# The gates' low one-hot tiles of the first token half, made by ScalarE instead of VectorE

## The chip, the cores and the metric

The kernel is one launch on one core of a Trainium2 chip. The metric is the device time of that launch in microseconds (us). The profile shows the engines by short names: PE (TensorE, matrix products), PEld (its weight loads), DVE (VectorE), ACT (ScalarE), POOL (GpSimd) and SP (the queue that issues most transfers).

## What is computed

One layer of a transformer on 1024 tokens of width 1024: attention in windows, a short convolution, gated merging, and then a layer of 16384 experts ("PEER"). For the change only the last part matters, cut to this:

```python
s = einsum('thpd,hpnd->thpn', qh, sub_keys)            # 8 heads, 2 key halves, 128 keys
s_top, i_top = top_k(s, 16)
cand = s_top[:, :, 0, :, None] + s_top[:, :, 1, None, :]
best, pos = top_k(cand, 16)                            # 8 x 16 = 128 experts for each token
idx = i1 * 128 + i2
g = softmax(best)
act = gelu(ue . t)                                     # rows of u_tab picked by idx
out = sum_k (g * act)_k * ve_k                         # rows of v_tab picked by idx
```

For most tokens the kernel runs every expert densely, and so it needs the gates as a dense table: for each token a 128 by 128 matrix G with G[i2, i1] equal to the sum of g over the token's 128 picks (i1, i2). One token's G is a product of two one-hot matrices: E2 (pick by i2) transposed, times E1 (pick by i1) scaled by the gate g of the pick.

## The kernel before

The 1024 tokens are two halves of 512, called half 0 and half 1 (`hf`). Half 0 is the first half. The stage that matters is woven from two streams by `run_side`: the main stream `stage2(1)` (gates, merging, mixing, normalization, queries and scores of half 1, most of it matrix products of 512 columns into PSUM banks) and the side stream `gates(0)`, which makes the gate tables of half 0. A scheduler then sets the order of instructions on each engine by readiness and its own costs, so a changed instruction moves others. Each engine runs its own list strictly in order.

`gates(0)` runs four times (one for each 128 tokens) a selection and a build. `select` works almost only on VectorE: the 16 best of the candidates by maximum, index and replace instructions, then four rounds of a comparison tile `eq`, whose second factor `fe` ScalarE widens. `slots` turns the three results (i1, i2, gate) on TensorE, so that picks lie on partitions and tokens on the free axis, and ScalarE copies them out as `ii` and `g16`.

`build_g` takes 8 tokens at a time (a round, 16 rounds in a build). For each round VectorE makes four float16 tiles of 128 by 1024: `e1` and `e2` (comparison of a ramp with i1 and i2, both named `e` in the rows), `ah` (e1 times the high part of the gate) and `al` (e1 times the low part; the gate is kept as two float16 numbers). `expand` then multiplies: for each token two products of 128 columns (e2 by ah, e2 by al), four tokens to a PSUM bank `fbank` of which there are two, and ScalarE evicts each bank into `ge`, 512 columns at a time. Every 16 tokens `ge` goes to memory by a transfer that GpSimd issues. The tiles e1, e2, ah and al have two buffers each.

In the main stream the names are: `sa` and `sgv` (ScalarE evicts sigmoids, VectorE multiplies them, GpSimd adds `sa`), `mh` and `ml` (halves of the merged result: ScalarE, GpSimd), `x` (residual), `sq` (squares: ScalarE, added up by GpSimd), `rstd` (reciprocal root), `h2h` and `h2l` (the normalized activations), `qqh`/`qql` (queries), `sl` (scores), `sv`/`si` (their 16 best). The tail of the stage is the maximum and index work of `scores` on VectorE; the dense expert loop begins with the product `ups` when the last `sl` has been evicted.

Of the kernel before, what the change touches and what calls it, by code (L numbers as in the profile page):

```python
# [8 lines left out]
F32 = mybir.dt.float32  # L9
F16 = mybir.dt.float16  # L10
# [3 lines left out]
AF = mybir.ActivationFunctionType  # L14
ALU = mybir.AluOpType
# [12 lines left out]
TB = 8  # L28
REP = 4
# [80 lines left out]
class K:  # L110
# [828 lines left out]
    def slots(self, t, hf):  # L939

        nc, p = self.nc, self.pg
        fig = self.sel[hf, t][1]
        pt = self.fbank()
        for i in range(3):
            nc.tensor.transpose(pt[:, i * 128:(i + 1) * 128], fig[:, i, :], self.id32)
        ii = p.tile([128, 256, REP], F16, name="ii", tag="ii", bufs=1)
        nc.scalar.activation(ii, pt[:, 0:256].unsqueeze(2).to_broadcast([128, 256, REP]), AF.Copy)
        g16 = p.tile([128, 2, 128, REP], F16, name="g16", tag="g16", bufs=1)
        self.split(pt[:, 256:384].unsqueeze(2).to_broadcast([128, 128, REP]), 4096.0, g16[:, 0], g16[:, 1])
        return ii.rearrange("p (a b) r -> p a b r", a=2), g16  # L950

    def build_g(self, t, hf):

        nc, p = self.nc, self.pg
        yield
        yield
        ii, g16 = self.slots(t, hf)
        yield
        late = []
        for q in range(128 // 16):  # L960
            ge = p.tile([128, 128, 16], F32, name="ge", tag="ge", bufs=self.ge_bufs)
            for sub in range(16 // TB):
                t0 = q * 16 + sub * TB
                ts = slice(t0, t0 + TB)

                def onehot(name, src, idx, op):
                    x = p.tile([128, TB, 128 // REP, REP], F16, name=name, tag=name, bufs=2)
                    nc.vector.tensor_tensor(x, src, idx[:, ts].unsqueeze(2).to_broadcast([128, TB, 128 // REP, REP]),
                                            op=op)
                    return x  # L970

                e1 = onehot("e1", self.iota, ii[:, 0], ALU.is_equal)
                ah = onehot("ah", e1, g16[:, 0], ALU.mult)
                al = onehot("al", e1, g16[:, 1], ALU.mult)
                e2 = onehot("e2", self.iota, ii[:, 1], ALU.is_equal)
                late.append((t, hf, q, sub, ge, ah, al, e2))
                if len(late) > 1:
                    self.expand(*late.pop(0))
                yield
        for x in late:  # L980
            self.expand(*x)
            yield
# [465 lines left out]
```

## Time and profile before

| | |
|---|---|
| median of 3 runs | 3120.34 us (3112.7 to 3122.46) |
| the profiled execution | 3120.57 us, span 3118.8 us |
| PE busy | 2913.7 us, 93% of the span |
| DVE busy | 2631.9 us, 84% |
| ACT busy | 1180.7 us, 38% |
| POOL busy | 1067.5 us, 34% |
| the changed stage (first `ii` to the first `ups`) | 740 to 1111 us |

The table shows averages over stages that differ. What the changed stage waits for has to be read in that stage; its length adds to the rest, since the dense loop behind it starts when it is over.

### The profile page before, as it was taken

What the parts mean: (1) busy time and instruction counts of PE and PEld (TensorE: products, weight loads), DVE (VectorE), ACT (ScalarE), POOL (GpSimd) and SP (SyncE); (2) the same over time, 40 slices, a digit from 0 to 9 for tenths busy, and PEclk for the clock granted to TensorE, in tenths of its full rate; (3) what the DMA queues carried; (4) which work ended last, traced back from release to release, by engine and by line L of the source; (5) the groups of instructions that cost most, each with busy time, mean ns of one, the idle gap of its engine ahead of it and who ended that gap; (6) DMA issues with size and microseconds to landing.
All of it is one profiled execution on the core that took longest, in us unless ns stands there. A gap on an engine that the chain in (4) does not pass through costs nothing. (4 is left out here: it accounts for less than half of the span.)

```text
span 3118.8 us, 49200 instructions
## 1 busy us (share of the span) xinstructions
PE 2913.7 (93%) x18685; PEld 1534.6 (49%) x18685; DVE 2631.9 (84%) x5438; ACT 1180.7 (38%) x1878; POOL 1067.5 (34%) x812
## 2 busy tenths in 40 slices
PE   6899999998899989999999999999999999999998
PEld 2455555444454444443444444344444456666665
DVE  7788666698899999899799988889988988777687
ACT  4744566333444332322333332333332333433332
POOL 2100011202231004444444544444444443444453
PEclk9999999999999999999999999999999999999999
DMA  6333334653445628898899998889898989999996
GB/s 218 95 110 111 112 116 152 234 183 136 174 191 196 234 87 307 280 317 303 303 316 335 345 325 297 295 318 342 315 335 304 336 287 341 328 323 326 333 321 225
DMA packets 327198, 795.75 MB, mean 255 GB/s; under 512 B 22961, under 2 KB 147249, under 8 KB 319793
## 3 DMA queue, kind: packets, MB, share of 16 engines
q1 hardware_dynamic: 222992, 397.25, 38.1%
q0 software_dynamic: 103968, 395.36, 34.8%
q8 instruction: 146, 2.39, 0.3%
q14 instruction: 92, 0.75, 0.1%
HBM read 696.31 MB, written 96.21 MB: 254 GB/s over the span
## 5 line engine op out<-in xcount | busy, mean ns | idle before, releaser
L904 POOL DMA_INDIRECT row<-u,ci x512 | 680.5, 1329 | 920.9 <-DVE row L67 685.0
L67 DVE SCALAR_TENSOR_TENSOR row<-row,hn 128x1024 f32<-128x1024 f32 x512 | 620.6, 1226 | 80.9 <-DMA row<-u,ci 75.0
L67 PE MATMUL res<-wdl,vh 128*128 128x128 f16 (+2 forms) x2176 | 629.3, 306 | 28.1 <-DVE wdl L67 28.0
L67 PEld LDWEIGHTS <-vh 128*128 128x128 f16 x5120 | 469.2, 98 | 340.0 <-issue 11.3
L67 PE MATMUL res<-wdh,vh 128*128 128x128 f16 (+2 forms) x2176 | 625.1, 306 | 3.3 <-ACT vh L1109 1.7
L67 PE MATMUL res<-wdh,vl 128*128 128x128 f16 (+2 forms) x2176 | 625.7, 306 | 0.8 <-DVE vl L67 0.8
L67 PE MATMUL ups<-h,uh 128*128 128x512 f16 x1952 | 589.8, 384 | 21.9 <-DVE acc L67 12.8
L67 PEld LDWEIGHTS <-whl 128*128 128x128 f16 x3288 | 315.1, 99 | 367.9 <-issue 41.9
L1109 ACT ACTIVATE vh<-v 128x1024 f16<-128x1024 f32 x248 | 258.4, 1052 | 484.9 <-DMA v<-v 433.6
L67 PE MATMUL ups<-h,ul 128*128 128x512 f16 x976 | 374.9, 384 | 21.1 <-DVE ul L67 21.1
L67 PE MATMUL bank<-hT,whl 128*128 128x512 f16 x1584 | 375.5, 386 | 15.7 <-ACT hT L331 5.7
L67 PEld LDWEIGHTS <-vl 128*128 128x128 f16 x2560 | 251.5, 98 | 205.0 <-issue 37.2
L67 DVE SCALAR_TENSOR_TENSOR vl<-v,vh 128x1024 f16<-128x1024 f32 x248 | 300.1, 1222 | 55.6 <-ACT vh L1109 53.1
L67 PEld LDWEIGHTS <-uh 128*128 128x128 f16 x1952 | 192.8, 99 | 258.0 <-issue 36.6
L904 POOL DMA_INDIRECT row<-v,ci x128 | 200.5, 1566 | 220.8 <-DVE racc L67 197.7
L140 ACT ACTIVATE uh<-u 128x1024 f16<-128x1024 f32 x122 | 128.4, 1052 | 311.1 <-PE ups L67 255.3
L1128 ACT ACTIVATE wdh<-gel 128x512 f16<-128x512 f32 x128 | 80.3, 629 | 371.4 <-DVE gel L67 353.3
L67 DVE SCALAR_TENSOR_TENSOR racc<-row,fig,racc 128x1024 f32<-128x1024 f32 x127 | 163.0, 1283 | 10.7 <-DMA row<-v,ci 9.7
L67 PEld LDWEIGHTS <-ul 128*128 128x128 f16 x976 | 96.6, 99 | 141.6 <-DVE ul L67 23.5
L67 DVE SCALAR_TENSOR_TENSOR ul<-u,uh 128x1024 f16<-128x1024 f32 x122 | 148.6, 1221 | 15.2 <-ACT uh L140 15.1
L67 PEld LDWEIGHTS <-e 128*128 128x128 f16 x1792 | 114.4, 99 | 94.4 <-issue 37.5
L67 DVE TENSOR_TENSOR e<-iotas,ii 128x1024 f16<-128x1024 f16 x224 | 145.4, 691 | 18.2 <-PE fbank L67 13.1
(230 smaller groups left out, 4192.6 us busy)
## 6 DMA issues: line engine op xcount, KB each, us to landing
v<-v SPq DMA_DIRECT2D x248, 512.0 KB, 6.5
u<-u_t SPq DMA_DIRECT2D x122, 512.0 KB, 6.7
gd<-ge POOLq DMA_DIRECT2D x32, 1024.0 KB, 4.4
gt<-gd SPq DMA_DIRECT2D x32, 1024.0 KB, 13.6
wm<-w_mod SPq DMA_DIRECT2D x48, 512.0 KB, 4.3
gd<-ge SPq DMA_DIRECT2D x24, 1024.0 KB, 8.6
gt<-gd SPq DMA_DIRECT2D x32, 768.0 KB, 11.0
w<-w_in SPq DMA_DIRECT2D x34, 512.0 KB, 4.2
```

Of the source, the lines that this page charges most:

```text
L67: r = f(*args, **kw)
L140: nc.scalar.activation(h, src, AF.Copy, scale=float(scale))
L904: self.nc.gpsimd.indirect_dma_start(out=r, out_offset=None, in_=tab, in_offset=bass.IndirectOffsetOnAxis(ap=ci[:, s:s + 1], axis=0))
L1109: nc.scalar.activation(vh, v32, AF.Copy, scale=16.0)
L1128: nc.scalar.activation(wh, ge, AF.Copy, scale=256.0)
```

## The change

For half 0 alone the low tile `al` is no longer one VectorE instruction for 8 tokens but eight ScalarE instructions, one for each token: a copy of 128 columns of e1, with the token's low part (`glo`, float32, one number for each partition) as the scale. `glo` is computed once for each build from 128 columns, where `g16`'s low half took 512. Half 1, built later beside the dense loop, is as before.

```diff
         g16 = p.tile([128, 2, 128, REP], F16, name="g16", tag="g16", bufs=1)
-        self.split(pt[:, 256:384].unsqueeze(2).to_broadcast([128, 128, REP]), 4096.0, g16[:, 0], g16[:, 1])
+        wide = pt[:, 256:384].unsqueeze(2).to_broadcast([128, 128, REP])
+        if hf:
+            self.split(wide, 4096.0, g16[:, 0], g16[:, 1])
+        else:
+            self.glo = p.tile([128, 128], F32, name="glo", tag="glo", bufs=2)
+            nc.scalar.activation(g16[:, 0], wide, AF.Copy, scale=4096.0)
+            self.lo(self.glo, pt[:, 256:384], 4096.0, g16[:, 0, :, 0])
...
                 e1 = onehot("e1", self.iota, ii[:, 0], ALU.is_equal)
                 ah = onehot("ah", e1, g16[:, 0], ALU.mult)
-                al = onehot("al", e1, g16[:, 1], ALU.mult)
+                if hf:
+                    al = onehot("al", e1, g16[:, 1], ALU.mult)
+                else:
+                    al = p.tile([128, TB, 128 // REP, REP], F16, name="al", tag="al", bufs=2)
+                    for u in range(TB):
+                        nc.scalar.activation(al[:, u], e1[:, u], AF.Copy, scale=self.glo[:, t0 + u:t0 + u + 1])
                 e2 = onehot("e2", self.iota, ii[:, 1], ALU.is_equal)
```

The scheduler's order moves with it. In the first build ScalarE (names: `g` is g16, `ii` the turned indices) had, before:

```order
L947 ACTIVATE ii<-fbank 128x1024
L140 ACTIVATE g_7630<-fbank 128x512
L715 ACT_TABLE_LOAD
L715 ACTIVATE sa<-bank 128x512
L994 ACTIVATE ge<-fbank 128x128x4 x6
L720 ACTIVATE sgv<-bank 128x512
L994 ACTIVATE ge<-fbank 128x128x4 x14
```

and has now:

```order
L947 ACTIVATE ii<-fbank 128x1024
L954 ACTIVATE g_7630<-fbank 128x512
L985 ACTIVATE al<-e_7668,glo 128x128 x8
L985 ACTIVATE al<-e_7683,glo 128x128 x8
L1005 ACTIVATE ge<-fbank 128x128x4 x2
L985 ACTIVATE al<-e_7719,glo 128x128 x8
L1005 ACTIVATE ge<-fbank 128x128x4 x2
L715 ACT_TABLE_LOAD
L715 ACTIVATE sa<-bank 128x512
L985 ACTIVATE al<-e_7784,glo 128x128 x8
L1005 ACTIVATE ge<-fbank 128x128x4 x2
```

Eight `al` stand ahead of every pair of `ge`, and the `al` of a round stand ahead of the `ge` of the round before it; the table load and `sa` come after two rounds.

On VectorE the fourth selection stood behind the third build (`fi` and `cand` begin a selection, `x` is the residual):

```order
L67 TENSOR_TENSOR ah<-e_9879,g_9332 128x1024
L67 TENSOR_TENSOR al<-e_9879,g_9332 128x1024
L67 TENSOR_TENSOR e_9908<-iotas,ii 128x1024
L67 TENSOR_TENSOR e_9914<-iotas,ii 128x1024
L67 TENSOR_TENSOR ah<-e_9908,g_9332 128x1024
L67 TENSOR_TENSOR al<-e_9908,g_9332 128x1024
L67 SCALAR_TENSOR_TENSOR x_9435<-bank,g1s,x_9435 128x512
L67 CAST fi<-si_3544 128x256
L67 TENSOR_TENSOR cand<-sv_3543 128x8x16
```

Now it stands inside the build, from its fifth round on:

```order
L67 TENSOR_TENSOR e_9750<-iotas,ii 128x1024
L67 CAST fi<-si_3544 128x256
L67 TENSOR_TENSOR cand<-sv_3543 128x8x16
L67 TENSOR_TENSOR cand<-sv_3543 128x8x8
L67 TENSOR_TENSOR cand<-sv_3543 128x8x5
L67 TENSOR_TENSOR cand<-sv_3543 128x8x4
L67 TENSOR_TENSOR cand<-sv_3543 128x8x3
L67 TENSOR_TENSOR ah<-e_9750,g_9558 128x1024
L67 TENSOR_TENSOR e_9763<-iotas,ii 128x1024
L67 TENSOR_TENSOR cand<-sv_3543 128x8x2 x3
L67 TENSOR_TENSOR cand<-sv_3543 128x8x8
L67 MAX best<-cand 128x8
```

All of the maximum and index work of the fourth selection, to the first `eq`, now lies between tiles of the third build; the second and the third selection still stand behind the build before them.

In the fourth build ScalarE had, in the middle of the build before:

```order
L994 ACTIVATE ge<-fbank 128x128x4 x2
L799 ACTIVATE hn<-bank 128x512
L994 ACTIVATE ge<-fbank 128x128x4 x8
L799 ACTIVATE hn<-bank 128x512
L994 ACTIVATE ge<-fbank 128x128x4 x6
L140 ACTIVATE qqh<-bank 128x512
L810 ACTIVATE sl<-bank 128x512
L994 ACTIVATE ge<-fbank 128x128x4 x4
L799 ACTIVATE hn<-bank 128x512
L994 ACTIVATE ge<-fbank 128x128x4 x4
L140 ACTIVATE qqh<-bank 128x512
```

and now, for about the same rounds:

```order
L1005 ACTIVATE ge<-fbank 128x128x4 x2
L331 ACTIVATE h2h_10541<-x_9683,b2s 128x512 x3
L799 ACTIVATE hn<-bank 128x512
L1005 ACTIVATE ge<-fbank 128x128x4 x2
L140 ACTIVATE qqh<-bank 128x512 x2
L985 ACTIVATE al<-e_11057,glo 128x128 x8
L985 ACTIVATE al<-e_11093,glo 128x128 x8
L1005 ACTIVATE ge<-fbank 128x128x4 x2
L985 ACTIVATE al<-e_11129,glo 128x128 x8
L1005 ACTIVATE ge<-fbank 128x128x4 x2
L985 ACTIVATE al<-e_11165,glo 128x128 x8
L1005 ACTIVATE ge<-fbank 128x128x4 x2
```

All eight `h2h` stood ahead of this build; now four are inside it, three of them here, and the evictions of the main stream (`hn`, `qqh`, `sl`) stand between groups of `al`.

On TensorE the products of 512 and 128 columns of the main stream between the first and the last one-hot product are, build by build, 95, 95, 102 and 149 before and 169, 141, 90 and 180 now. In the first build and most of the second ten of them stand between the sixteen one-hot products of one round and those of the next (six before). The third build has none in its last seven rounds and the fourth none in six rounds in its middle. Between the sums of the squares and the last turn (`slots`) ahead of the fourth build stand 34 products of 512 columns now.

## Rows read from the trace of the kernel before

**Rows 1.** Windows: from:to, length, busy PE PEld DVE ACT POOL, granted clock, DMA share, GB/s.

```profile
740.00:787.00 47.00, 39.97 (x346) 23.69 (x345) 40.32 (x67) 20.63 (x37) 13.78 (x9) 0.93 0.47 180
787.00:815.00 28.00, 25.08 (x132) 11.79 (x130) 26.05 (x113) 10.58 (x15) 5.28 (x5) 1.00 0.47 170
815.00:862.00 47.00, 40.45 (x347) 23.96 (x346) 40.73 (x69) 20.08 (x36) 13.98 (x10) 0.93 0.48 181
862.00:888.00 26.00, 23.98 (x123) 11.12 (x121) 24.95 (x112) 9.65 (x14) 3.12 (x4) 1.00 0.46 168
888.00:936.00 48.00, 43.27 (x361) 25.58 (x362) 44.83 (x70) 21.49 (x38) 20.74 (x11) 0.96 0.53 204
936.00:982.00 46.00, 40.73 (x191) 18.68 (x190) 42.15 (x132) 20.52 (x29) 8.54 (x6) 0.93 0.49 166
982.00:1028.00 46.00, 43.68 (x412) 26.41 (x411) 45.82 (x101) 23.21 (x43) 3.76 (x7) 1.00 0.67 246
1028.00:1111.00 83.00, 69.53 (x462) 36.82 (x461) 83.00 (x454) 30.00 (x44) 0.53 (x1) 0.96 0.59 195
```

**Rows 2.** Timeline, all engines, one round of the first build (start, duration in us).

```profile
747.36 0.69 DVE L67 TENSOR_TENSOR ah<-e,g 128x1024 f16<-128x1024 f16 x1
...
747.97 0.69 DVE L67 TENSOR_TENSOR al<-e,g 128x1024 f16<-128x1024 f16 x1
...
748.57 1.29 DVE L67 TENSOR_TENSOR e<-iotas,ii 128x1024 f16<-128x1024 f16 x2
...
749.29 1.09 ACT L994 ACTIVATE ge<-fbank 128x512 f32<-128x512 f32 x2 [1.32 <-PE fbank L67]
...
749.77 0.69 DVE L67 TENSOR_TENSOR ah<-e,g 128x1024 f16<-128x1024 f16 x1
```

**Rows 3.** Groups by line, 725 to 1030 us: busy us, mean ns, idle before.

```profile
L994 ACT ACTIVATE ge<-fbank 128x512 f32<-128x512 f32 x128 | 69.7, 594 | 75.8 <-PE fbank L67 65.2 <-DMA gd<-ge 6.5 <-issue 1.1
...
L67 DVE TENSOR_TENSOR al<-e,g 128x1024 f16<-128x1024 f16 x64 | 44.1, 689 | 0.0
```

**Rows 4.** Groups by line and shape, ScalarE, whole span.

```profile
L331 ACT ACTIVATE h2h<-x,b2s 128x512 f16<-128x512 f32 x8 | 5.7, 719 | 5.2 <-DVE x L67 5.1
...
L331 ACT ACTIVATE hc<-x,b 128x256 f16<-128x256 f32 x8 | 3.5, 498 | 3.8 <-DVE x L67 3.6
...
L892 ACT ACTIVATE fig<-fig 128x128 f32<-128x128 f32 x8 | 2.5, 307 | 0.3 <-DVE fig L67 0.2
```

**Rows 5.** Timeline of ScalarE: short instructions back to back, and a table load.

```profile
79.78 1.30 ACT L331 ACTIVATE hc<-x,b 128x256 f16<-128x256 f32 x3 [2.57 <-DVE x L67]
...
87.54 2.39 ACT L426 ACTIVATE rt<-bank 32x512 f32<-32x512 f32 x4
...
741.22 1.28 ACT L715 ACT_TABLE_LOAD   x1
...
972.78 1.32 ACT L331 ACTIVATE h2h<-x,b2s 128x512 f16<-128x512 f32 x2
```

**Rows 6.** Timeline, first build's stall and one GpSimd addition behind a selection.

```profile
766.80 8.86 POOL L727 TENSOR_TENSOR sa<-sa,sgv 128x512 f32<-128x512 f32 x1 [3.55 <-DVE sgv L67]
...
775.68 0.63 ACT L728 ACTIVATE mh<-sa 128x512 f16<-128x512 f32 x1 [8.45 <-POOL sa L727]
...
780.47 0.69 DVE L67 TENSOR_TENSOR e<-iotas,ii 128x1024 f16<-128x1024 f16 x1 [5.94 <-PE fbank L67]
...
811.93 1.37 POOL L727 TENSOR_TENSOR sa<-sa,sgv 128x512 f32<-128x512 f32 x1 [14.11 <-DVE sgv L67]
```

**Rows 7.** Timeline of TensorE before and at the first one-hot products.

```profile
739.49 4.26 PE L67 MATMUL bank<-hT,whl 128*128 128x512 f16 x19
...
743.89 0.90 PEld L67 LDWEIGHTS <-e 128*128 128x128 f16 x16 [0.64 <-DVE e L67]
```

**Rows 8.** Timeline, second normalization of the second half.

```profile
956.26 2.07 PE L67 MATMUL bank<-sq,ones 128*128 128x512 f32 x2 [4.84 <-POOL sq L314]
...
963.32 3.35 DVE L67 RECIPROCAL rstd<-rstd 128x512 f32<-128x512 f32 x1 [3.03 <-ACT rstd L323]
```

## The prediction

> **What bounds the kernel now.** The table of windows comes first, because the change is confined to one stage. Its edges are cut at the starts of `ii` (740, 815, 888, 982), at VectorE's last instruction of each build (787, 862, 936, 1028) and at the first `ups` (1111). The reader is to see two kinds of stretches in [rows 1]. In the builds ScalarE is busy under half of the time (20.6 of 47 us) and VectorE 40 to 46 of 46 to 48. In the last 83 us VectorE never rests. So VectorE sets the pace nearly everywhere from 740 to 1111; ScalarE and TensorE follow.
>
> The timeline of one round shows how [rows 2]. From one `ah` to the next are 2.41 us, made of four VectorE instructions that follow each other at 0.60 us (each lasts 0.69 and overlaps the next). In the same 2.41 us ScalarE does two evictions, 1.09 us, and then waits for TensorE. Sixteen rounds are 38.6 us of a build's 47; the rest is a lead-in and a stall, which the next view explains. Late in the first build GpSimd adds `sa` for 8.86 us, where the same addition takes 1.37 beside another mix of VectorE work; ScalarE's next instruction, `mh`, waits 8.45 us for it; the evictions behind `mh` on ScalarE wait too, the banks stay full, and VectorE stands still for 5.94 us [rows 6]. The second build has a stall like it, the third a smaller one.
>
> **The change part by part.**
>
> *Removed.* 64 `al` on VectorE, 44.1 us of busy time [rows 3], at a pitch of 0.60 us 38.6 us of its time; and three quarters of four wide splits, under half a microsecond each. Where VectorE alone sets the pace, a round would go from 2.41 to 1.81 us.
>
> *Added.* 512 ScalarE instructions of 128 columns with a scale read from memory. No row has this form, so it is bounded. From below: a 128-column instruction without such an operand takes 0.307 us [rows 4]; two `h2h` of 0.719 end after 1.32 [rows 4, 5], so the second starts 0.60 after the first and 0.12 is overlapped; 0.307 less 0.12 is 0.19. From above: `hc`, 256 columns with an operand from memory, takes 0.498; `h2h`, 512 columns, 0.719 [rows 4]; that is 0.86 ns for a column, so 128 columns take 0.39, and four `rt` in 2.39 us, 0.60 each, show ScalarE instructions that hardly overlap [rows 5]. Between: three `hc` in 1.30 us [rows 5] follow each other at (1.30 - 0.498)/2 = 0.40, two `h2h` at 0.60; 0.78 ns for a column, so 128 columns follow at 0.40 - 0.10 = 0.30. I take 0.30, since `hc` is the nearest row in length, operand and place (on-chip memory to on-chip memory, all partitions).
>
> *A round now.* Two evictions follow each other at 0.50 us (1.09 less one of 0.594 [rows 2, 3]), 1.0 for the pair. ScalarE needs 8 x 0.30 + 1.0 = 3.4 us, VectorE 1.8. TensorE needs at most ten main products at (4.26 - 0.4)/18 = 0.215 and sixteen one-hot ones at 0.90/16 = 0.056 [rows 7], 3.05 us. ScalarE becomes the pace of the builds. The products of a round wait for its `al`, but `ge` of that round stands behind the next round's `al`, 2.4 us later, so ScalarE itself does not wait for TensorE.
>
> The Trainium skill speaks against the change: its page "ScalarE: Activation LUTs", in "Rules for kernel authors", sends multiplications to VectorE. The rows say the same of the price (2.4 us against 0.6 for a round); what the rule would make of the whole is the second rival below, whose number comes from rows.
>
> *First build.* About 2 us pass from the start of `ii` to the first `al` (`ii`, one `e`, `glo`; the first one-hot product stood 3.9 us in, at 743.89 [rows 7]). Then 16 x 3.4 = 54.4. On ScalarE also stand a table load of 1.28 [rows 5] and five evictions of 0.5 of the main stream: 4. VectorE is done before ScalarE: with two buffers its last tiles go in when the fourteenth `al` is done, and ScalarE then has two groups of `al` and four pairs of `ge` left, 8.8, of which VectorE uses 2; so the next selection starts 7 us ahead of ScalarE's end. 2 + 54 + 4 - 7 = 53, against 47: **+6**. The stall of 5.94 us is gone in this: VectorE is busy in only half of the time, `mh` stands three rounds behind `sgv`, and even 8.86 us for `sa` would fit. *Second build*, without the table load and with three evictions: 51 against 47, **+4**. The selections behind both are VectorE's (26.05 of 28, 24.95 of 26 [rows 1]) and keep their length; `fe` on ScalarE is wanted only after the maximum work, by the same estimate as below some 14 us in.
>
> *Third build and what follows (888 to 982, 94 us).* The maximum work of the fourth selection now stands inside this build, where VectorE has 3.4 - 1.8 = 1.6 us to spare in each round, 26 us in all, so the part of a selection's 26 us that is ahead of the first `eq`, which I put at 15 (the four `eq` rounds and the gates' division are the rest), is hidden. The build ends for ScalarE at 2 + 54 + 1 = 57. Then the main stream's normalization: four squares and their GpSimd additions (to about 63), the sum on TensorE of 2.07 us, the root, the reciprocal of 3.35 [rows 8], and the 34 main products that stand ahead of the last turn, 34 x 0.215 = 7.3. I put the next `ii` at 78: **-16**. The wait of 4.84 us for the last square and that of 3.03 for the root [rows 8] remain in some form.
>
> *Fourth build.* The lead-in has three main evictions more (1.3), the build ten or eleven that sit between groups of `al` (6 or 7 us), and at two places (`qqh` behind three `h2h`, and `qqh` again four rounds later) ScalarE waits for up to 18 main products, 3.9 us, of which I count 5 in all. 2 + 1 + 54 + 7 + 5 = 69 to ScalarE's end; VectorE does a group of score work, 5 us, in the wait and is done about 8 before: 61, against 46: **+15**. *Tail:* the same fifteen groups of scores, and two splits (`vl`, `ul`) more ahead of it: **+2**. Nothing else in the dense loop moves; it starts later by the sum.
>
> *Sum.* 6 + 4 - 16 + 15 + 2 = +11 on the profiled 3120.6, which is also the median: **3131**.
>
> **The rivals.** A run of this kernel can tell about 0.3%, 9.4 us, from no change.
>
> *First rival, faster.* The operand from memory costs nothing when instructions follow each other, and `al` comes at 0.19. Then ScalarE needs 2.5 a round, TensorE's ten products hold about half of the rounds at 3.05, and a round saves 0.35 to 0.9, some 9 us a build: 11 - 36 = -25, **3096**. For: `ge` shows that the fixed part is mostly overlapped. Against: `hc` at 0.40 for 256 columns. It decides from 0.26 down (each 0.01 is 16 x 8 x 4 x 0.01 = 5 us).
>
> *Second rival, the rule as it stands.* Nothing is given back: 64 rounds longer by 1.0 us, and the third selection's hiding and the stalls buy nothing because the main stream, in order behind the waiting products, is late by as much: **3184**. The same time comes from `al` at 0.39 with all gains kept, 11 + 46 and a little. For: `rt` does not overlap. Against: VectorE's 38.6 us are real, and 15 us of selection have moved into idle time.
>
> *Third rival, a slower TensorE.* In the third build TensorE has only 0.9 us of work in each of the last seven rounds, in the fourth in six. Where it idled before, behind the last square, the granted clock of 936 to 982 fell to a mean of 0.93, against 1.00 in the selections [rows 1, 8]. If it goes to the lower level there, the 34 products and the next 50 or so cost twice 0.215, 18 us more on the chain to the fourth build: **3150**. For: those rows. Against: the one-hot products come at every round.
>
> *Fourth rival, no change.* The last build's lag hides behind the scores: from 982 to 1111 VectorE is busy for 128.8 of 129 us [rows 1], and with 16 x 0.6 taken off and some ten normalization instructions of 0.66 and the two splits put on, its own work is as long as before. If ScalarE's waits there fall beside score groups, the 17 of the last two terms shrink to 0 to 8: **3115 to 3123**.
>
> **How the numbers follow.** The forecast has 0.45 (its own range 3122 to 3142), the fourth rival 0.2, the first 0.15, the third 0.13, the second 0.07. About a third of the forecast lies within 9.4 us of no change, with it most of the fourth rival: 0.32 the same. Faster 0.18: the first rival and a little of the fourth. Slower 0.50. From 3104 to 3155 leaves out half of the first rival, the second and a little more.
>
> **What would show it.** In the changed kernel's profile: `al` of 128 columns at a pitch of 0.30 (right between 0.28 and 0.32); a round of 3.4 us with ScalarE without gaps, and VectorE about half busy in the builds; no `mh` wait of 8 us; the stretch from the third to the fourth `ii` near 78 us; the tail's VectorE still full. The prediction is wrong if `al` comes at under 0.26 or near 0.39, if the fourth build is not over 55 us, or if the dense loop changes its length.

## The result and the profile after

The changed kernel takes 3138.36 us (median of 12 runs, 3127.51 to 3150.45) against 3120.05 for the kernel before (12 runs on the same chip, 3111.41 to 3126.33). The ratio is 1.0063 with a 95% interval of 1.0047 to 1.0080: it is slower, by about 20 us (0.6%). The forecast was 3131 with a range of 3104 to 3155. The profiled execution took 3135.03 us, its span is 3133.3.

The windows of the changed kernel answer to [rows 1], cut in the same way: at the four `ii`, at VectorE's last tile of each build, at the first `ups`. Three more windows inside the last two builds follow.

```profile
738.80:791.00 52.20, 51.85 (x393) 29.62 (x392) 34.77 (x52) 51.70 (x151) 6.11 (x8) 0.97 0.51 187
791.00:820.70 29.70, 25.20 (x130) 11.97 (x129) 26.55 (x112) 16.79 (x31) 5.94 (x6) 0.89 0.42 151
820.70:872.00 51.30, 48.63 (x375) 28.37 (x374) 34.29 (x52) 50.81 (x152) 6.07 (x8) 0.97 0.51 186
872.00:904.70 32.70, 25.42 (x132) 11.62 (x131) 30.41 (x115) 14.83 (x28) 8.82 (x8) 0.95 0.40 145
904.70:952.00 47.30, 38.77 (x318) 24.32 (x317) 44.36 (x134) 46.83 (x141) 3.23 (x6) 0.91 0.43 174
952.00:983.00 31.00, 16.97 (x89) 9.58 (x87) 21.61 (x36) 22.86 (x42) 7.36 (x6) 0.64 0.45 162
983.00:1049.00 66.00, 54.97 (x440) 34.45 (x439) 44.68 (x97) 59.98 (x170) 3.75 (x7) 0.87 0.50 183
1049.00:1135.20 86.20, 74.78 (x495) 39.84 (x494) 86.20 (x454) 33.93 (x55) 0.53 (x1) 0.98 0.65 217
...
945.00:975.00 30.00, 13.77 (x89) 10.09 (x89) 19.29 (x34) 25.41 (x57) 7.89 (x7) 0.51 0.46 176
...
1010.00:1025.00 15.00, 10.71 (x72) 7.82 (x71) 5.26 (x8) 13.28 (x37) 1.59 (x3) 0.50 0.43 169
```

ScalarE's busy time in a build went from 20.6 of 47 us to 51.7 of 52.2: it is the pace now, and VectorE's is 34.8. The stage ends 24.7 us later (first `ups` at 1135.21, before at 1110.56). By the time from one `ii` to the next that is 81.9, 84.0, 78.2 us and 152.3 to `ups`, where before it was 74.9, 73.8, 93.3 and 128.8: +7, +10, -15, +23.5. Some 10 of the 24.7 came back behind it, in the dense loop of this execution: from the first `ups` to the end of the span are 1998 us, before 2008. In the profiles of the other kernels, whose dense loop is written the same, this part is 1991 to 2015 us long, so it is not read further.

The timeline of the changed kernel, ScalarE, VectorE, GpSimd and TensorE, at the places that answer to [rows 2, 6, 8]:

```profile
740.79 4.78 ACT L985 ACTIVATE al<-e,glo 128x128 f16<-128x128 f16 x16 [0.47 <-DVE glo L67]
...
754.92 2.44 ACT L985 ACTIVATE al<-e,glo 128x128 f16<-128x128 f16 x8
757.26 1.06 ACT L1005 ACTIVATE ge<-fbank 128x512 f32<-128x512 f32 x2
758.21 2.44 ACT L985 ACTIVATE al<-e,glo 128x128 f16<-128x128 f16 x8
...
756.31 0.69 DVE L67 TENSOR_TENSOR ah<-e,g 128x1024 f16<-128x1024 f16 x1 [1.53 <-PE fbank L67]
...
762.90 1.64 POOL L727 TENSOR_TENSOR sa<-sa,sgv 128x512 f32<-128x512 f32 x1 [3.74 <-DVE sgv L67]
...
887.09 0.63 ACT L728 ACTIVATE mh<-sa 128x512 f16<-128x512 f32 x1 [5.32 <-POOL sa L727]
887.79 1.22 POOL L729 TENSOR_TENSOR ml<-sa,mh 128x512 f16<-128x512 f32 x1 [0.74 <-ACT mh L728]
888.04 1.52 DVE L67 TENSOR_TENSOR eq<-eq,fe 128x1024 f16<-128x1024 f16 x1
889.66 1.05 ACT L872 ACTIVATE fe<-fi 128x1024 f16<-128x1024 f16 x1 [1.94 <-DVE eq L67]
...
962.10 1.22 DVE L67 TENSOR_TENSOR eq<-eq,fe 128x1024 f16<-128x1024 f16 x1 [7.49 <-ACT fe L872]
...
970.49 2.08 PE L67 MATMUL bank<-sq,ones 128*128 128x512 f32 x2 [10.51 <-POOL sq L314]
974.27 7.52 PE L67 MATMUL bank<-h,whl 128*128 128x512 f16 x34
...
1019.85 1.99 ACT L331 ACTIVATE h2h<-x,b2s 128x512 f16<-128x512 f32 x3
...
1022.51 1.06 PE L67 MATMUL bank<-h2h,whl 128*128 128x512 f16 x2
...
1025.70 0.60 ACT L140 ACTIVATE qqh<-bank 128x512 f16<-128x512 f32 x1 [2.42 <-PE bank L67]
...
1026.37 0.59 PE L67 MATMUL bank<-h2h,whl 128*128 128x512 f16 x2
```

The kernel before had, in its second selection:

```profile
870.76 0.63 ACT L728 ACTIVATE mh<-sa 128x512 f16<-128x512 f32 x1 [5.58 <-POOL sa L727]
...
876.31 0.69 DVE L67 TENSOR_TENSOR eq<-eq,fe 128x1024 f16<-128x1024 f16 x1
877.04 1.05 ACT L872 ACTIVATE fe<-fi 128x1024 f16<-128x1024 f16 x1 [2.65 <-DVE eq L67]
```

Sixteen `al` take 4.78 us, one alone 0.416 (the mean of 512), so they follow each other at (4.78 - 0.416)/15 = 0.29 us. From `al` group to `al` group are 3.29 us (754.92 to 758.21) without a gap on ScalarE, and VectorE waits for banks in between. GpSimd's addition in the build is down from 8.86 us to 1.64, and `mh` finds it done. In the second selection `mh` waits 5.32 us ahead of a `fe` (5.31 at 806.00 in the first). That wait is not new, before it was 5.58 us at the same place, and it does not hold the selection: in both kernels the `fe` behind it waits on for VectorE's `eq`.

### The profile page after: what moved, and what is told of

Read it like the earlier page. It is cut to its first block, busy times and chain, and to the rows that moved or that the text cites. A ratio compares the mean times of both kernels' runs of the same rounds, so it can differ in the third digit from the quotient of the medians.

```text
span 3133.3 us, 49683 instructions
## 1 busy us (share of the span) xinstructions
PE 2925.8 (93%) x18685; PEld 1545.8 (49%) x18685; DVE 2602.9 (83%) x5374; ACT 1321.1 (42%) x2390; POOL 1040.5 (33%) x812
## 4 chain that ended last, share of the span: by engine, by line
issue 24%; PE 22%; DVE 21%; POOL 13%; DMA 11%; ACT 8%; POOLq 0%; DVEq 0%; SPq 0%; ACTq 0%
POOL row L904 12%; PE bank L67 11%; PE res L67 5%; PE sc L67 4%; ACT al L985 4%; DMA row<-u,ci 3%; DMA v<-v 3%; DVE row L67 3%; DMA gt<-gd 2%; DVE si L67 2%; ACT ge L1005 2%; DVE vl L67 2%; DVE eq L67 1%; DVE racc L67 1%; DVE sv L67 1%
## 5 line engine op out<-in xcount | busy, mean ns | idle before, releaser
L904 POOL DMA_INDIRECT row<-u,ci x512 | 687.6, 1343 | 916.6 <-DVE row L67 681.8
L67 PE MATMUL fbank<-ah,e 128*128 128x128 f16 x896 | 124.0, 227 | 44.4 <-ACT ge L1005 24.8
```

Of the source, the lines that this page charges most:

```text
L67: r = f(*args, **kw)
L904: self.nc.gpsimd.indirect_dma_start(out=r, out_offset=None, in_=tab, in_offset=bass.IndirectOffsetOnAxis(ap=ci[:, s:s + 1], axis=0))
```

## The experiments

The theory: ScalarE, at 3.3 us for a round, became the pace of the builds, and only in the third build is this given back, where a selection fills VectorE's idle time. The rivals: the moved order (waits of `mh`, `fe`, `h2h` and `qqh` behind others on ScalarE), relief of VectorE that is worth nothing since the main stream sets the end, and TensorE's lower clock.

Executions of one kernel spread by about 10 us to each side; the ratios below are medians of several runs with their 95% intervals. The stage itself, read from one profile, is finer. The table gives for every kernel the starts of the third and the fourth `ii`, of the sum of squares of half 1 on TensorE (S, the product of `sq` with ones, the row at 970.49 above; before: 956.26 in [rows 8]), of the first query eviction `qqh` and of the first `ups`, in us. The first `ii` itself starts between 736.9 and 739.9 us in these profiles, so differences of up to 3 us in the table need not be the stage's. A "period" below is the time from one `ii` to the next, or from the fourth to the first `ups`.

| kernel | al on ScalarE | third ii | S | fourth ii | first qqh | first ups | ratio to before |
|---|---|---|---|---|---|---|---|
| before | none | 888.4 | 956.3 | 981.7 | 983.6 | 1110.6 | 1 |
| changed | all four builds | 904.7 | 970.5 | 982.9 | 1025.7 | 1135.2 | 1.0063 |
| third only | 3 | 889.0 | 957.4 | 971.0 | 1005.4 | 1114.6 | 1.0009 (0.9994 to 1.0025) |
| fourth only | 4 | 887.8 | 956.5 | 981.6 | 983.5 | 1126.8 | 1.0054 (1.0034 to 1.0073) |
| first two | 1, 2 | 902.6 | 958.9 | 985.0 | 986.8 | 1113.8 | 1.0011 (0.9994 to 1.0028) |
| first three | 1, 2, 3 | 902.3 | 968.1 | 980.6 | 1016.5 | 1125.4 | 1.0061 (1.0037 to 1.0085) |
| last two | 3, 4 | 887.8 | 956.2 | 969.9 | 1010.7 | 1120.7 | 1.0040 (1.0023 to 1.0056) |
| four and four | half, in all | 885.9 | 953.5 | 978.1 | 979.9 | 1107.0 | 0.9996 (0.9982 to 1.0011) |
| constant scale | all, no operand | 882.1 | 942.4 | 967.4 | 969.1 | 1101.6 | 0.9975 (0.9957 to 0.9993) |
| unused copies | VectorE, copies | 907.3 | 974.6 | 987.1 | 1028.3 | 1139.3 | 1.0086 (1.0060 to 1.0112) |
| no al | nobody | 878.4 | 942.2 | 966.8 | 968.6 | 1092.2 | 0.9945 (0.9926 to 0.9963) |
| before, VectorE sum | none | 883.2 | 942.4 | 968.4 | 970.3 | 1097.3 | 0.9937 (0.9916 to 0.9958) |
| four and four, VectorE sum | half, in all | 872.6 | 941.6 | 967.1 | 968.9 | 1097.0 | 0.9939 (0.9918 to 0.9960) |
| changed, VectorE sum | all four builds | 903.7 | 968.2 | 982.7 | 1023.7 | 1136.7 | 1.0061 (1.0037 to 1.0084) |

### The price: a constant scale, unused copies, four and four, no low tile

*Constant scale:*

```diff
-                        nc.scalar.activation(al[:, u], e1[:, u], AF.Copy, scale=self.glo[:, t0 + u:t0 + u + 1])
+                        nc.scalar.activation(al[:, u], e1[:, u], AF.Copy, scale=0.001)
```

> As the changed kernel, but the scale is the constant 0.001 and no number read from memory; this leaves the low parts' values out of the result. By the theory al then comes at a pitch of 0.20-0.22 us (a memory operand costs about 0.08 on each), a round is 8 x 0.21 + 1.0 = 2.7 us or, where TensorE's ten main products bound it, 3.05, and the run is 20 to 40 us faster than the changed kernel: 3098 to 3118. By the rival that ScalarE is not the pace, or that the operand costs nothing when instructions follow each other, al stays near 0.29 or the rounds near 3.3, and the time within 6 us of the changed kernel, 3138.

Measured: 3108.2 us. The timeline of ScalarE in this kernel's first build:

```profile
746.46 1.70 ACT L985 ACTIVATE al<-e 128x128 f16<-128x128 f16 x8
748.06 1.07 ACT L1005 ACTIVATE ge<-fbank 128x512 f32<-128x512 f32 x2
749.01 1.71 ACT L985 ACTIVATE al<-e 128x128 f16<-128x128 f16 x8
```

A round is 2.55 us, and eight `al` take 1.70 instead of 2.44. With one alone at 0.34 (the mean of this kernel's 512) they follow at (1.70 - 0.34)/7 = 0.19 to 0.20. The memory operand thus costs 0.09 us even when instructions follow each other, and taking it away moves the stage's end from 1135.2 to 1101.6. Part of that can be the order: here the scheduler has all eight `h2h` ahead of the fourth `ii`, as in the kernel before. The Trainium skill's page "ScalarE: Activation LUTs", section "What ACT_TABLE_LOAD costs", gives 186 ns + 0.833 ns for a column, 93 ns more for each operand read per partition, and 93 ns of overlap between instructions in a row; an estimate by it is 0.29 us with the operand and 0.20 without, and the trace agrees with both.

*Unused copies:* `al` is VectorE's again, and ScalarE makes the same copies for nobody.

```diff
+                al = onehot("al", e1, g16[:, 1], ALU.mult)
...
-                    al = p.tile([128, TB, 128 // REP, REP], F16, name="al", tag="al", bufs=2)
+                    dum = p.tile([128, TB, 128 // REP, REP], F16, name="dum", tag="dum", bufs=1)
                     for u in range(TB):
-                        nc.scalar.activation(al[:, u], e1[:, u], AF.Copy, scale=self.glo[:, t0 + u:t0 + u + 1])
+                        nc.scalar.activation(dum[:, u], e1[:, u], AF.Copy, scale=self.glo[:, t0 + u:t0 + u + 1])
```

> VectorE makes al as before in all four builds, and ScalarE also makes the same eight copies a round into a tile that nobody reads (work added, nothing taken away): the cost of ScalarE's time without the relief of VectorE. A round asks ScalarE for 3.3 us and VectorE for 2.4. By the theory (ScalarE's 3.3 us is the pace, the relief of VectorE is worth something only in the third build and around the selections) the builds of this kernel are as long as those of the changed one, 1 to 3 us apart, the third selection is hidden less since VectorE has 0.9 us instead of 1.5 to spare in a round, and the run takes 3140 to 3160 us. By the rival that the relief of VectorE was worth nothing at all, the time is that of the changed kernel within 4 us, 3134 to 3142; by the rival that the products' wait for al on the slower engine is what costs, and not ScalarE's time, this kernel is at 3118 to 3126, since its products wait for VectorE alone.

Measured: 3145.46 us; the periods are 81.4, 86.4, 79.8 and 152.2 us, those of the changed kernel within 2.4. All of VectorE's relief is worth 4 us at the end of the stage (1139.3 against 1135.2). The loss comes with the copies on ScalarE, and the rival on the products' wait falls. The copies bring both their time and the order that the scheduler makes around them (six of eight `h2h` stand behind the fourth `ii` here and in the changed kernel); in no run does one stand without the other, so the two are not separated.

*Four and four:* ScalarE makes four tokens' `al`, VectorE the other four.

```diff
-            nc.scalar.activation(g16[:, 0], wide, AF.Copy, scale=4096.0)
+            self.split(wide, 4096.0, g16[:, 0], g16[:, 1])
...
-                    for u in range(TB):
+                    for u in range(4):
                         nc.scalar.activation(al[:, u], e1[:, u], AF.Copy, scale=self.glo[:, t0 + u:t0 + u + 1])
+                    nc.vector.tensor_tensor(al[:, 4:], e1[:, 4:], g16[:, 1, t0 + 4:t0 + TB].unsqueeze(2).to_broadcast(
+                        [128, TB - 4, 128 // REP, REP]), op=ALU.mult)
```

> In all four builds ScalarE makes four tokens of the eight of each low tile, VectorE the other four in one instruction of 512 columns; the split of the wide tile is back, glo is kept. A round asks ScalarE for 4 x 0.29 + 1.0 = 2.2 us and VectorE for 3 x 0.6 + 0.35 = 2.15. By the theory (ScalarE's pace is the cause) a round takes 2.2 to 2.45 us, a build no longer than before, the third selection is not hidden, and the run takes 3110 to 3122 us. By the rival that it is the order (instructions of the main stream queued behind groups of al on ScalarE) and not the pace that costs, the builds stay 5 to 10 us longer than before and the run takes 3130 or more.

Measured: 3116.5 us, no difference from the kernel before. A round takes 2.12 us (the pairs of `ge` at 750.10 and 752.22), 0.29 less than before, but sixteen rounds of that would be 4.6 us for a build and the first two periods are 73.0 and 74.3, against 74.9 and 73.8. The timeline of GpSimd and ScalarE in the first build of this kernel shows where it went:

```profile
764.01 7.46 POOL L727 TENSOR_TENSOR sa<-sa,sgv 128x512 f32<-128x512 f32 x1 [0.58 <-DVE sgv L67]
...
771.50 0.63 ACT L728 ACTIVATE mh<-sa 128x512 f16<-128x512 f32 x1 [4.64 <-POOL sa L727]
```

VectorE has hardly a pause in these rounds, GpSimd's addition takes 7.46 us again, and `mh` waits for it ahead of ScalarE's evictions: the stall of [rows 6].

*No low tile:* the second product of each token takes `ah`; the low part of the gates is left out of the result.

```diff
-            self.glo = p.tile([128, 128], F32, name="glo", tag="glo", bufs=2)
...
-            self.lo(self.glo, pt[:, 256:384], 4096.0, g16[:, 0, :, 0])
...
-                    al = p.tile([128, TB, 128 // REP, REP], F16, name="al", tag="al", bufs=2)
-                    for u in range(TB):
-                        nc.scalar.activation(al[:, u], e1[:, u], AF.Copy, scale=self.glo[:, t0 + u:t0 + u + 1])
+                    al = ah
```

> al isn't made at all, on no engine; the second product of each token takes ah again (the low parts are left out of the result, the products on TensorE stay in number). VectorE has 1.8 us a round, ScalarE 1.0. By the theory (the main stream's point of the second half's sum of squares, and the fourth build, set the stage's end) the sum of squares starts at 935 to 943 us, where the kernels with a fast GpSimd sum had it, the fourth build is 4 to 10 us shorter than before, and the run takes 3085 to 3103. By the rival that VectorE's work alone sets the end, 64 x 0.6 us come off and the run takes 3078 to 3085; by the rival that only GpSimd's additions count, 3098 to 3104.

Measured: 3101.82 us. S at 942.2 is as the theory had it; from the fourth `ii` to `ups` it is 125.4 us, only 3.4 shorter than before, where 4 to 10 were expected. The time cannot tell the theory from the rival on GpSimd's additions (they take 1.64 us here), but the rival that VectorE's work alone sets the end falls: 38.6 us off VectorE bring 18.

### One build at a time

The five kernels differ in one condition, written for the fourth build here and in the same way for the others:

```diff
-        if hf:
+        if hf or t != 3:
...
-                if hf:
+                if hf or t != 3:
```

> Only the fourth build makes its low tiles on ScalarE. By the theory the first four ii stand as before, the fourth ii to the first ups grows from 129 to 148-153 us, and the run takes 3135 to 3143 us: most of the loss of the whole change in one build. By the rival that the loss of the fourth build is inherited (main stream late from the third build, a slow TensorE clock around the fourth selection, waits of the query evictions moved by the other builds), the fourth build has no such lag when the first three are as before: 129 to 137 us, 3120 to 3128.

Measured: 3134.09 us, the first `ups` 16.2 us later, nothing moved ahead of the fourth `ii`. The fourth build costs that by itself, and the rival falls.

> Only the third build makes its low tiles on ScalarE; the other three builds are as before. By the theory (ScalarE at 3.3 us a round is the pace of a build, and only where VectorE has work to put into its idle time is it given back) the first ii to the third stay at 74 to 75 us apart, the third ii to the fourth falls from 93.3 to 78-80 us, the fourth build stays at 46-48, and the run takes 3103 to 3110 us. By the rival that the whole stage's main stream is late by as much as ScalarE is (nothing is hidden), the third ii to the fourth stays at 92-95 and the time within 5 us of the kernel before, 3120.

Measured: 3122.33 us, and the time is where the rival had it, though the mechanism of the theory is there: the fourth `ii` comes at 971.0, 11 us earlier than before (82.0 us after the third; 78 to 80 had been expected). From there to `ups` it is 143.6 instead of 128.8. The timeline of ScalarE in this kernel says why:

```profile
968.75 2.38 ACT L331 ACTIVATE h2h<-x,b2s 128x512 f16<-128x512 f32 x3 [0.99 <-DVE x L67]
971.04 1.02 ACT L947 ACTIVATE ii<-fbank 128x1024 f16<-128x1024 f32 x1
...
1003.17 0.72 ACT L331 ACTIVATE h2h<-x,b2s 128x512 f16<-128x512 f32 x1 [1.55 <-DVE x L67]
1005.44 0.60 ACT L140 ACTIVATE qqh<-bank 128x512 f16<-128x512 f32 x1 [1.54 <-PE bank L67]
```

and that of the kernel before has, at the same place:

```profile
980.30 1.52 ACT L331 ACTIVATE h2h<-x,b2s 128x512 f16<-128x512 f32 x2 [2.40 <-DVE x L67]
981.73 1.02 ACT L947 ACTIVATE ii<-fbank 128x1024 f16<-128x1024 f32 x1
983.60 0.62 ACT L140 ACTIVATE qqh<-bank 128x512 f16<-128x512 f32 x1
```

Before, all eight `h2h` stood ahead of the fourth `ii`, and the first query followed it. With the selection hidden, the build comes earlier than the rest of the normalization: five `h2h` stand inside it, and the first query is 22 us later than before. The chain that ends the stage is the main stream's (normalization, queries, scores), and it did not get shorter.

> Only the first and the second build make their low tiles on ScalarE. By a sum over the builds (each build's loss stands for itself) the two periods grow by 7 and 10 us as in the changed kernel, the rest stays, and the run is 15 to 18 us slower than the kernel before: 3133 to 3138. By the rival that the main stream, which advances while the side stream waits, makes the longer builds good (third-only lost 15 us in the fourth build that it had won in the third), the third ii to the first ups becomes shorter than the 222 us of before by 8 to 15 us and the run is 2 to 8 us slower: 3120 to 3127.

Measured: 3121.77 us. The first two periods grow to 81.4 and 84.0 as in the changed kernel, and 14 us late at the third `ii` are 3.2 at the first `ups`: the rival holds, the sum over builds falls. The third build, VectorE's here, has its period at 82.4 us with no selection hidden. The main stream, whose last `ml` came at 885.6 (before 890.5), has less to do beside it.

From these, a reading in two parts was made ahead of the next two runs: the time to S, and that from S to the first `ups`.

> The first three builds make al on ScalarE, the fourth on VectorE. By the two-part reading (the stage is the time to the second half's sum of squares, 14.2 us later in the changed kernel, and from there to the first ups, 154 us or 157 where only the third build is ScalarE's) the sum of squares starts at 969 to 972 us, the rest takes 154 to 159, the first ups comes 15 to 19 us later than before, and the run takes 3131 to 3138. By a sum over single builds (the fourth alone cost 16.4 of 24.6) the first ups comes 6 to 9 us later: 3124 to 3129.

Measured: 3137.86 us, S at 968.1, from there 157.3 us. That is the two-part reading, at or just under its lower bounds: it had S at 969 or later and the first `ups` 15 to 19 us late (14.8 measured), and not the 6 to 9 of the sum. Its median equals the changed kernel's although its stage ends 10 us earlier; what the dense loop gives back there is within the spread of executions.

> The third and the fourth build make al on ScalarE, the first two on VectorE. By the two-part reading the sum of squares starts at 957 to 959 us as in third-only, the rest takes 163 to 166 as in the changed kernel, the first ups comes 9 to 13 us later than before, and the run takes 3127 to 3133. By a sum over single builds (+4 and +16.4) the first ups comes 19 to 21 us later: 3136 to 3141.

Measured: 3130.38 us, S at 956.2 (957 expected), from there 164.5 us, the first `ups` 10.1 us late. The two-part reading again, and not the 19 to 21 of the sum.

### The sum on GpSimd

The stall of [rows 6] was still what four-and-four lost to. So VectorE makes the sum of half 1, first in the kernel before:

```diff
-            nc.gpsimd.tensor_tensor(sa, sa, sv, op=ALU.add)
+            (nc.vector if hf else nc.gpsimd).tensor_tensor(sa, sa, sv, op=ALU.add)
```

> The kernel before, with VectorE instead of GpSimd for the sum sa + sgv of half 1, and no other change. The stall of 5.9 us in the first build and the one like it in the second go, three VectorE instructions of 0.6 us come in each of the two periods. By the theory the first two periods fall from 74.9 and 73.8 to 69-72 us and the run takes 3108 to 3116; by the rival that VectorE's work sets the stage's end, 3117 to 3124.

Measured: 3100.53 us, the ratio 0.9937. It is faster than both kernels, and by more than the theory's 4 to 12 us. The timeline of VectorE and ScalarE in the first build:

```profile
764.50 0.69 DVE L67 TENSOR_TENSOR sa<-sa,sgv 128x512 f32<-128x512 f32 x1
...
765.31 0.63 ACT L728 ACTIVATE mh<-sa 128x512 f16<-128x512 f32 x1
```

The first two periods fall only to 73.3 and 72.5 (69 to 72 said); the gain appears later. The last `ml` is out at 875.2 instead of 890.5, S comes at 942.4 instead of 956.3, and from S to `ups` it is 154.9, as before. The stage gives 13.3 of the 20 us (1097.3 against 1110.6), the lower end of what the interval of the ratio allows (13 to 26 us); where the rest would come from no run shows.

> As the four-and-four kernel, and VectorE instead of GpSimd makes the sum sa + sgv of half 1 (eight instructions of 0.6 us). In four-and-four a round takes 2.12 us, 0.29 less than before, but ScalarE's mh waits 14.4 and 18.7 us for GpSimd's sa in the first two periods, where the changed kernel had no long wait of mh in a build. By the theory that this wait gives back what the shorter rounds win, the first two periods fall from 73.0 and 74.3 to 66-70 us and the run takes 3102 to 3112. By the rival that VectorE's whole work (scores, splits made early) sets the stage's end, the periods shrink and the fourth build or the tail grows by as much: 3113 to 3121.

Measured: 3098.43 us. The periods fall to 66.4 and 68.5 as by the theory (of the waits named there the second is 15.0 us and not 18.7, which counts one of 3.77 twice), but S and `ups` come when they come without the four-and-four split (941.6 and 1097.0): the third `ii` is 10.6 us earlier, and the period after it 9.2 us longer. So the time below the theory's 3102 is the sum's: moving half of `al` to ScalarE is worth nothing measurable on top of it.

> The changed kernel, with VectorE instead of GpSimd for the sum sa + sgv of half 1. In the kernel before, this took 8.9-us additions out of two builds and 20 us off the run. In the changed kernel the additions in the builds take 1.64 us already, and mh waits 13.5 us for GpSimd in the first two periods, most of it in the selections (5.3 us twice, fe behind it). By the theory that the change has already had the gain of the fast additions, and loses on ScalarE's pace, this kernel gains 3 to 9 us on the changed one: 3129 to 3135. By the rival that the loss of the changed kernel lies in the new wait of mh and fe in the selections, it falls by 12 us or more, to 3126 or less.

Measured: 3137.91 us, so both expectations fall: there is no gain at all. `mh` waits 13.8 us for VectorE's sum in the first two periods, as it had waited 13.5 for GpSimd's. So the wait comes from where `mh` stands in ScalarE's order, not from the engine that adds. Since the wait stays, the time does not decide on the rival that puts the loss there; the traces do, as the `fe` behind `mh` waits for `eq` in this kernel too (1.99 us at 888.43). And the gain of a fast addition in the builds, the changed kernel already had.

## Why the prediction was right, and where not

*The price of `al` and the round* were right: 0.29 us (0.30 said), 3.29 us (3.4 said), ScalarE without gaps. VectorE is two thirds busy in the builds, not half, since the main stream's instructions stand there too. *First build:* +7 (+6 said). The stall is gone as said; the forecast had room for an addition of 8.86 us, and it takes 1.64.

*Second build:* +10 (+4 said). The step that failed is that the selections "keep their length". From the `ii` to VectorE's last tile the build is 51.7 us long (820.7 to 872.4), before 47.2, which is the +4 of the forecast. From there to the next `ii` it is 32.3 us, before 26.6, and that is VectorE's own work: it is busy for 30.41 us there (872.00 to 904.70), before for 24.95 (862 to 888, [rows 1]). Three residuals `x` of 0.75 us now stand in the selection, since the main stream is further on, and at four places VectorE's instructions take 0.8 to 1.0 us longer while a GpSimd instruction runs, like the `eq` with `fe` above: 1.52 us beside `ml`, 0.69 before.

*Third build and what follows:* the -16 came out as -15, with the selection hidden: from S to the fourth `ii` it is 12.4 us instead of 25.5. S itself is 14.2 us late: on ScalarE the last five squares and a `fe` stand behind the third build's `al`, the first of them at 958.35, and VectorE waits 7.49 us for that `fe`. The step that counted the -16 as a gain of the whole failed. Third-only shows the same advance of the fourth `ii` lost again behind it, because five of eight `h2h` then stand inside the fourth build. And first-two shows a period of 82.4 with nothing hidden, because the main stream was ahead.

*Fourth build and tail:* +23.5 (+17 said). Fourth-only has +16.2, so the term was right for a build that begins with the normalization done; the 7 us more go with the normalization that now lies behind the fourth `ii`, where VectorE waits 4.6 us for an `h2h`, 3.6 for a `qqh` and 5.2 for an `sl`. That is read from the waits; no run has it apart.

*The sum* is the step that was wrong in kind: terms from `ii` to `ii` are not additive, as two streams share one order on each engine and what one loses the other uses. Alone, the first two builds cost 3.2 us at `ups` (17 by their periods), the third 4.0 (-11 by its period), the fourth 16.2. That these three add up to 23.4, near the 24.7 of the whole, is chance: the first three builds cost 14.8 together and not 7.2, the last two 10.1 and not 20.2. What holds in all five mixtures is the two-part reading: S is 12 to 14 us late only where the first, the second and the third are all ScalarE's (the side stream is 14 to 16 us late at the third `ii`, and a third build at ScalarE's pace doesn't make it good); from S to `ups` it is 154 to 157 us with VectorE's fourth build, 164 to 165 with ScalarE's fourth behind a hidden selection, 170 with ScalarE's fourth alone. For the changed kernel: 14.2 + 10.4 us, the 24.7 of the stage, of which the runs show about 20. So the forecast's +11 was under half of what the stage lost; that the time still came within 8 us of 3131 is in part luck, as the dense loop gave some of it back within its spread.

*The rivals.* The first, `al` at 0.19, did not come; the constant scale shows its mechanism, at 3108 instead of 3096. The second, 3184, was too dark, but its reason was in part the right one: the main stream is late with ScalarE, and relief on VectorE is worth little (4 us in unused-copies). The rule of the Trainium skill's page that it named, "ScalarE: Activation LUTs", "Rules for kernel authors" (multiplications on VectorE), is borne out in its sign. The third came true in its condition: the granted clock is 0.51 from 945 to 975 and 0.50 from 1010 to 1025, the lower level (1.2 GHz), each time where ScalarE holds the one-hot rounds and there are few main products. Its price did not come. The 34 products behind S take 7.52 us, 0.22 each, since the clock is back by then (mean 0.98 from 974 to 983), and the rounds keep ScalarE's 3.29 us at the lower level too (`al` groups at 948.49 and 951.78). What stands on the path at the lower level is small: the second pair of sums behind S takes 1.89 us, before 1.02, and nine products ahead of the first query follow each other at 0.43 us instead of 0.22 (the pairs at 1022.51 and 1026.37). An estimate from these is 3 us, not 18; no run held the clock up with all else unchanged. The fourth rival fell with fourth-only.

## What to carry to other kernels

An engine that idles for half of a stage need not be able to take a share of the work: price the instruction at the pitch in which a row of them would follow, operands included, and add what the engine already does in a round. When two streams are woven, a period won or lost in one is not the stage's; find the chain that ends the stage and ask for each change whether it moves that chain's points (here S and the first query). And a short wait of an in-order engine for a slow helper, here eight additions on GpSimd, can be worth nearly as much as a quarter of VectorE's work on the tiles: 0.9937 for the sum and 0.9945 for no `al` at all, at the end of the stage 13.3 and 18.4 us.

## What the runs showed of the hardware

GpSimd's addition of two 128x512 float32 tiles, the same instruction in all kernels, takes 1.26 us beside a selection, 1.64 or 1.65 in builds where VectorE pauses (changed kernel, constant scale, no al; 3.44 once in unused copies), 7.46 in four-and-four and 8.86 in the builds before, where VectorE runs two-input 16-bit instructions back to back. The Trainium skill's page "SBUF — State Buffer", section "Who interferes with whom", has VectorE and GpSimd share a pair of ports as a lock that is held for a whole instruction, also for a two-input VectorE instruction on on-chip memory; the trace agrees in kind, and on GpSimd's side it is a stretching by up to seven times. VectorE can pay as well: in the selections of the changed kernel an instruction that meets one of GpSimd's is 0.8 to 1.0 us longer (1.52 us beside `ml`, 0.69 without), while in the builds of the kernel before, where GpSimd's addition takes 8.86 us, VectorE's tiles keep 0.69. VectorE's sum takes 0.69 us, and the additions of the squares show the same in the kernel before: mean 3.79 us there (888 to 1110), 1.53 in third-only.
